# A quarter of the weights' low parts made by ScalarE and an adding transfer in place of VectorE's subtraction

## The chip, the cores and the metric

The kernel runs on one core of a Trainium2 chip, and its time is the device time of one launch in microseconds. TensorE (PE in the profile; PEld is its weight load) multiplies matrices, VectorE (DVE), ScalarE (ACT) and GpSimd (POOL) do the rest, SyncE (SP) issues transfers. Each engine works through its own list of instructions in order and waits on semaphores where it needs another's result. A transfer that GpSimd issues goes through a queue of its own (q0 in the profile), one that SyncE issues through another (q1).

## The reference

One step of a two-layer trunk over 128 context tokens and 512 latent tokens, width 1024, all in float32. Cut to what matters here:

```
h = rms(x, norm1) * (1 + sc1) + sh1
proj = h @ w_in                      # 1024 -> 8464 columns, split below
qa, ka, va, ga, beta, alpha, qb, ib, fb, gb, q_c, k_c, v_c, mg = split(proj)
o_a = rms(gated_delta(q, k, v, ...)) * silu(ga)      # recurrence over chunks of 64
o_b = rms(hgrn2(silu(qb), ib, fb, ...)) * silu(gb)   # recurrence over chunks of 32
o_c = windowed_attention(q_c, k_c, v_c)
x = x + g1 * (sum_r sigmoid(mg_r) * (o_r @ w_branch_r)) @ w_out
h2 = rms(x, norm2) * (1 + sc2) + sh2
x = x + g2 * (silu(conv(h2 @ w_up_a)) * conv(h2 @ w_up_u)) @ w_down
```

## The kernel before

TensorE multiplies in a reduced format (float32r), so every product is made of three: activations and weights are each split into a high part, which the format holds exactly, and a low part, the rest. A step over 128 rows of a weight block (k_steps, line 969) does high weights x high activations, high weights x low activations, low weights x high activations, each in two pieces of 256 and 384 tokens.

Weights come in blocks of four such steps, 128 x 512 numbers, 256 KB. SyncE loads a block into wraw (w_issue, line 897), ScalarE copies it into whi in the reduced format, and VectorE subtracts: wlo = wraw - whi (the function go in w_queue, line 927). There are four buffers each of wraw, whi and wlo (NRAW and NHI, lines 41 and 42). A block's high part is queued once the block four before it has been used up, so TensorE has three other blocks to work on in the meantime; a raw buffer is loaded again once its block has been split. The blocks of the first three tiles of layer 1 and of each ConvFFN have buffers of their own (wx) and are split twelve blocks early (W_EARLY).

The program is written in one pass by a planner. Several streams (the projections as the main one; two for the delta recurrence, one for the other recurrence, and attention, norms and adaLN beside them) each hand out their next instructions. A model clock for each engine (_go, _ready) says when a stream could go on, and drive (line 512) takes a stream that is ready by TensorE's clock, or else the next projection step. So the order of every engine's list, TensorE's included, is fixed when the kernel is built, and depends on what the planner believes of each operation's cost. In a mixer the projections of w_in for the heads a0 a1 b0 a2 b1 a3 b2 b3 (MIX_ORDER, line 51) are the filler between the steps of the recurrences; then come the attention columns, the gates ga and gb, and the merge with mg. VectorE does the recurrences' elementwise work, the short convolutions (Cv) and the subtractions, all in one queue. POOL issues the spills of the context tokens' part (pspill), the loads of states and part of the adaLN weights, and sets a few buffers to zero.

Of the kernel before, what the change touches and what calls it, by code (L numbers as in the profile page):

```python
# [7 lines left out]
F32 = mybir.dt.float32  # L8
# [3 lines left out]
AF = mybir.ActivationFunctionType  # L12
ALU = mybir.AluOpType
# [19 lines left out]
ENGS = ("pe", "act", "dve", "pool")  # L33
# [3 lines left out]
PRIO = {"norm": -1, "ab": 0, "attn": 3, "ada": 4, "y": 0}  # L37
PRIO_MIX = ({"delta": 1, "delta1": 2, "hgrn": 2}, {"delta": 1, "delta1": 2, "hgrn": 2})
ADA_LATE = 3000.0
C_ROOM = (5, 5)  # L40
NRAW = 4
NHI = 4
# [15 lines left out]
IN_COL = {"q": 0, "k": 512, "v": 1024, "ga": 1536, "ab": 2048, "qb": 2064, "ib": 2576,  # L58
          "ff": 3088, "fb": 3600, "gb": 4112, "qc": 4624, "kc": 5136, "vc": 5264, "mg": 5392}
# [177 lines left out]
class Trunk:  # L237
# [181 lines left out]
    def dma(self, out, in_, queue="pool", fresh=False):  # L419

        load = self.in_sbuf(out)
        e, n = ENGS.index("pool"), len(ENGS)
        c = self._cells(out if load else in_)
        t = 0.0 if fresh else self._ready(e, [c] if load else [], [] if load else [c])
        t = max(self.clk[queue], t) + (1050.0 if queue == "pool" else 450.0)
        self.clk[queue] = t
        self.clk["dma"] = max(self.clk["dma"], t) + out.shape[0] * self._n(out) / 90.0
        t = self.clk["dma"] + 2000.0
        if load:
            c[e] = t  # L430
        else:
            np.maximum(c[n + e], t, out=c[n + e])
        (self.nc.gpsimd if queue == "pool" else self.nc.sync).dma_start(out=out, in_=in_)  # L433
        return t

    @staticmethod
    def in_sbuf(ap):
# [318 lines left out]
    def ada_rest(self, chunks, raws, accs, gap, done, after=None):  # L756
# [15 lines left out]
        for n, (l, j, k) in enumerate(steps):  # L772
# [10 lines left out]
            if k < KD - 1 or not q:  # L783
                continue
            self.cur.now += ADA_LATE
            yield None
# [3 lines left out]
            self.cp(ar, ps)  # L790
            self.cur.now += ADA_LATE
            yield None
# [115 lines left out]
    def w_queue(self):  # L908

        if self.w_queued == len(self.units):  # L910
            return False
        u = self.w_order[self.w_queued]
        key, _, _, kt, n, own = self.units[u]
        if own:
            if self.wx is None:
                return False
            hi, lo = self.wx[:, own - 1, 0], self.wx[:, own - 1, 1]
        else:
            if len(self.w_ring) >= NHI and self.w_ring[-NHI] >= self.w_free:
                return False  # L920
            self.w_ring.append(u)
            hi = self.rotating(self.wp, [128, 4, 128], "whi", NHI, F32R, bufs=NHI)
            lo = self.rotating(self.wp, [128, 4, 128], "wlo", NHI, F32R, bufs=NHI)
        n = max(n, 32)
        self.w_hl[u] = (hi, lo)

        def go():
            raw = self.w_rawt.pop(u)
            if n < 128:
                self.cp(hi[:, :kt, :n].bitcast(F32), raw[:, :kt, :n])  # L930
            else:
                self.cp(hi[:, :kt, :n], raw[:, :kt, :n])
                self.sub(lo[:, :kt, :n], raw[:, :kt, :n], hi[:, :kt, :n].bitcast(F32))
            self.w_done.add(u)

        self.w_pend.append(go)
        self.w_queued += 1
        return True
# [968 lines left out]
    def mixer(self, l, x):  # L1907
# [71 lines left out]
        def c_tiles():  # L1979
            yield self.room(2, C_ROOM[l], sl)  # L1980
            self.qc = [sl.pair(), sl.pair()]
            self.qcp = sl.half()
            self.kv = [sl.half() for _ in range(3)]
            self.spawn("attn", self.attention(l))
            for i, n in enumerate(("kc", "vc")):
                yield from self.mtile(("in", l, IN_COL[n]), self.hh, self.hl, KD)
                self.cp(self.s2(self.kv[i].ap), self.s_view(self.ps))
                self.cp(self.kv[2].c4[:, i], self.p_view(self.ps))
            self.post(("Ck", l))
            for j in range(4):  # L1990
                yield from self.mtile(("in", l, IN_COL["qc"] + j * 128), self.hh, self.hl, KD)
                self.cp(self.s2(self.qc[j // 2].ap[:, j % 2]), self.s_view(self.ps))
                self.cp(self.qcp.c4[:, j], self.p_view(self.ps))
            self.post(("Cq", l))
# [333 lines left out]
```

## Time and profile before

| | |
|---|---|
| time, median of 3 runs | 2674.06 us (2673.45 to 2674.49) |
| profiled execution, its own time | 2671.22 us |
| its span | 2669.4 us |
| TensorE busy | 2634.9 us, 99% |
| VectorE busy | 1843.0 us, 69% |
| ScalarE busy | 1130.8 us, 42% |
| POOL busy | 114.4 us, 4% |

A share of busy time is a mean over stages. Matmuls overlap, so a busy TensorE may still lose a few tenths of a microsecond at a time while its next weight load waits; the view of waits counts these by what ended them. "issue" is time in which an engine waited for nothing that the profile shows.

### The profile page before, as it was taken

What the parts mean: (1) busy time and instruction counts of PE and PEld (TensorE: products, weight loads), DVE (VectorE), ACT (ScalarE), POOL (GpSimd) and SP (SyncE); (2) the same over time, 40 slices, a digit from 0 to 9 for tenths busy, and PEclk for the clock granted to TensorE, in tenths of its full rate; (3) what the DMA queues carried; (4) which work ended last, traced back from release to release, by engine and by line L of the source; (5) the groups of instructions that cost most, each with busy time, mean ns of one, the idle gap of its engine ahead of it and who ended that gap; (6) DMA issues with size and microseconds to landing.
All of it is one profiled execution on the core that took longest, in us unless ns stands there. A gap on an engine that the chain in (4) does not pass through costs nothing.

```text
span 2669.4 us, 58665 instructions
## 1 busy us (share of the span) xinstructions
PE 2634.9 (99%) x23938; PEld 2534.1 (95%) x23938; DVE 1843.0 (69%) x4250; ACT 1130.8 (42%) x2577; POOL 114.4 (4%) x208
## 2 busy tenths in 40 slices
PE   8999999999999999999999999999999999999999
PEld 5999999999999999999999998999999999999999
DVE  6788865656765897988667888666564457546454
ACT  5555455544424432323345554645443334323232
POOL 1100110100000000000001001000000000000000
PEclk9999999999999999999999999999999999999999
DMA  8212222312444344444322112222222232222222
GB/s 270 73 40 58 65 75 80 112 53 60 134 132 131 100 141 154 151 149 148 108 77 75 44 49 63 65 71 66 56 64 68 76 115 68 77 74 69 83 74 81
DMA packets 365245, 243.49 MB, mean 91 GB/s; under 512 B 18069, under 2 KB 339137, under 8 KB 364848
## 3 DMA queue, kind: packets, MB, share of 16 engines
q1 hardware_dynamic: 355632, 213.70, 27.7%
q0 software_dynamic: 8912, 25.53, 2.9%
q8 instruction: 188, 3.08, 0.5%
q14 instruction: 81, 0.66, 0.1%
q10 hardware_dynamic: 432, 0.52, 0.1%
HBM read 225.79 MB, written 13.89 MB: 90 GB/s over the span
## 4 chain that ended last, share of the span: by engine, by line
PE 88%; DVE 7%; ACT 2%; issue 2%; DMA 1%; SPq 0%; ACTq 0%; DVEq 0%
PE mm L323 73%; PE sd L323 12%; PE sd L328 2%; DVE sl L358 1%; DVE ex L358 1%; DVE Cv L371 1%; ACT sl L348 1%; DMA ar<-in_ada_w_dram 1%; DVE acc L371 1%; DVE wlo L358 1%; DMA wraw<-in_w_up_dram 0%; DVE N L371 0%; SPq L433 0%; ACT ex L348 0%; DVE x L371 0%
## 5 line engine op out<-in xcount | busy, mean ns | idle before, releaser
L323 PE MATMUL mm<-hh,whi 128*128 128x256 f32 (+2 forms) x3696 | 868.7, 319 | 1.4 <-issue 0.7
L323 PE MATMUL mm<-hl,whi 128*128 128x256 f32 (+2 forms) x3696 | 840.4, 311 | 1.2 <-DVE hl L371 1.2
L323 PE MATMUL mm<-hh,wlo 128*128 128x256 f32 (+1 forms) x3632 | 834.8, 309 | 0.0
L323 PEld LDWEIGHTS mm<-hh,whi 128*128 128x128 f32 (+1 forms) x3696 | 646.1, 187 | 23.8 <-issue 15.4
L323 PEld LDWEIGHTS mm<-hl,whi 128*128 128x128 f32 (+1 forms) x3696 | 663.7, 187 | 4.0 <-DVE hl L371 1.8
L323 PEld LDWEIGHTS mm<-hh,wlo 128*128 128x128 f32 x3632 | 661.7, 188 | 0.0
L358 DVE TENSOR_TENSOR wlo<-wraw,whi 128x512 fp32r<-128x512 f32 x598 | 401.8, 681 | 302.6 <-ACT whi L348 301.8
L348 ACT ACTIVATE whi<-wraw 128x512 fp32r<-128x512 f32 x602 | 366.8, 618 | 306.7 <-PE mm L323 245.6
L371 DVE SCALAR_TENSOR_TENSOR Cv<-S,V,Cv 128x642 f32<-128x642 f32 x240 | 210.9, 886 | 2.3
L371 DVE SCALAR_TENSOR_TENSOR acc<-ar,cT,acc 128x512 f32<-128x512 f32 x252 | 176.8, 749 | 4.2 <-DMA ar<-in_ada_w_dram 4.0
L348 ACT ACTIVATE sl<-sl 128x512 f32<-128x512 f32 (+5 forms) x220 | 117.6, 545 | 143.5 <-DVE sl L358 103.3
L323 PE MATMUL mm<-fh,whi 128*128 128x256 f32 (+1 forms) x704 | 166.0, 311 | 1.8 <-DVE x L371 1.0
L323 PE MATMUL mm<-fl,whi 128*128 128x256 f32 (+1 forms) x704 | 165.0, 309 | 0.2
L323 PE MATMUL mm<-fh,wlo 128*128 128x256 f32 (+1 forms) x704 | 165.1, 309 | 0.0
L348 ACT ACTIVATE sl<-sd 128x512 f32<-128x512 f32 (+5 forms) x216 | 94.4, 451 | 161.7 <-PE sd L323 79.6
L323 PE MATMUL sd<-sl,sl 128*32 128x32 f32 (+4 forms) x3392 | 151.2, 228 | 6.3 <-DVE sl L358 5.1
L323 PEld LDWEIGHTS sd<-sl,sl 128*32 128x32 f32 (+3 forms) x3392 | 126.1, 129 | 26.8 <-issue 13.9
L358 DVE TENSOR_TENSOR sl<-sl,sl 128x512 f32<-128x512 f32 (+2 forms) x212 | 149.0, 741 | 3.3 <-ACT sl L348 2.0
L348 ACT ACTIVATE S<-mm 128x512 f32<-128x512 f32 x204 | 77.8, 434 | 155.0 <-PE mm L323 154.8
L371 DVE SCALAR_TENSOR_TENSOR x<-mm,mod,x 128x256 f32<-128x256 f32 (+1 forms) x192 | 74.6, 434 | 88.2 <-PE mm L323 83.8
L323 PEld LDWEIGHTS mm<-fh,whi 128*128 128x128 f32 x704 | 128.0, 189 | 4.2 <-issue 2.9
L323 PEld LDWEIGHTS mm<-fl,whi 128*128 128x128 f32 x704 | 128.1, 188 | 0.7 <-DVE fl L358 0.7
(280 smaller groups left out, 3121.6 us busy)
## 6 DMA issues: line engine op xcount, KB each, us to landing
wraw<-in_w_in_dram SPq DMA_DIRECT2D x264, 256.0 KB, 3.0
ar<-in_ada_w_dram SPq DMA_DIRECT2D x176, 256.0 KB, 3.5
wraw<-in_w_up_dram SPq DMA_DIRECT2D x176, 256.0 KB, 3.0
wraw<-in_w_down_dram SPq DMA_DIRECT2D x64, 256.0 KB, 3.0
wraw<-in_w_branch_dram SPq DMA_DIRECT2D x48, 256.0 KB, 3.0
wraw<-in_w_out_dram SPq DMA_DIRECT2D x32, 256.0 KB, 3.6
wraw<-in_w_down_dram SPq DMA_DIRECT2D x32, 192.0 KB, 2.6
x<-xspill POOLq DMA_DIRECT2D x16, 320.0 KB, 7.0
```

What stands on the lines that cost most here:

```text
L323: self.nc.tensor.matmul(out, lhsT, rhs, start=start, stop=stop)
L328: self.nc.tensor.transpose(out, in_, self.c_i[:k, :k])
L348: self.nc.scalar.activation(out=out, in_=in_, func=func, scale=scale, bias=bias, **kw)
L358: self.nc.vector.tensor_tensor(out, a, b, op=op)
L371: self.nc.vector.scalar_tensor_tensor(out=out, in0=a, scalar=s, in1=b, op0=op0, op1=op1)
```

## The change

For a weight block of w_in whose column lies ahead of the attention keys (columns of q, k, v, ga, qb, ib, ff, fb, gb and qc, without the first tile of q), the low part is made in another way: ScalarE writes the negative high part into wlo (a copy with scale -1.0), and a transfer issued by POOL adds the raw block to it in place. Everything else keeps the subtraction. Of the 616 blocks that are split, 152 in wlo and 4 in wx are of the new kind. In the planner's clock an addition costs POOL 1050 ns, and its result is there 2500 ns later.

```
+BY_DMA = ("in",)
...
+    def dma_add(self, out, in_):
+
+        e, n = ENGS.index("pool"), len(ENGS)
+        oc, ic = self._cells(out), self._cells(in_)
+        t = max(self.clk["pool"], self._ready(e, [oc], [ic])) + 1050.0
+        self.clk["pool"] = t
+        oc[e] = np.maximum(oc[e], t + 2500.0)
+        np.maximum(ic[n + e], t + 2500.0, out=ic[n + e])
+        self.nc.gpsimd.dma_start(out=out, in_=in_, accum_op=ALU.add)
...
                 self.cp(hi[:, :kt, :n], raw[:, :kt, :n])
-                self.sub(lo[:, :kt, :n], raw[:, :kt, :n], hi[:, :kt, :n].bitcast(F32))
+                if key[0] in BY_DMA and key[2] < IN_COL["kc"] and key[2] != IN_COL["q"]:
+                    self.act(lo[:, :kt, :n], raw[:, :kt, :n], AF.Copy, scale=-1.0)
+                    self.dma_add(lo[:, :kt, :n].bitcast(F32), raw[:, :kt, :n])
+                else:
+                    self.sub(lo[:, :kt, :n], raw[:, :kt, :n], hi[:, :kt, :n].bitcast(F32))
```

Since the planner's clocks differ, the lists of all engines are ordered a little differently. On VectorE, at the first short convolution of layer 0 (S0, S1 and Cv2 are its inputs, Cv0, Cv1 and Cv3 its sums, V the taps, sc_ the scalars of the delta recurrence), the list before reads:

```order
L376 TENSOR_SCALAR sc_t0_659<-sc_ab_655 128x40
L358 TENSOR_TENSOR wlo_814<-wraw_625,whi_813 128x512
L371 SCALAR_TENSOR_TENSOR Cv0_81<-S0_79,V_85,Cv0_81 128x642
L358 TENSOR_TENSOR sc_t0_659<-sc_t0_659,sc_ab_655 128x40
L371 SCALAR_TENSOR_TENSOR Cv1_82<-S1_80,V_85,Cv1_82 128x642
L371 SCALAR_TENSOR_TENSOR Cv0_81<-S0_79,V_85,Cv0_81 128x642
L371 SCALAR_TENSOR_TENSOR Cv1_82<-S1_80,V_85,Cv1_82 128x642
L358 TENSOR_TENSOR wlo_853<-wraw_715,whi_852 128x512
L376 TENSOR_SCALAR sc_t1_660<-sc_t0_659 128x40
L371 SCALAR_TENSOR_TENSOR Cv0_81<-S0_79,V_85,Cv0_81 128x642
L371 SCALAR_TENSOR_TENSOR Cv1_82<-S1_80,V_85,Cv1_82 128x642
```

And the same place now:

```order
L377 TENSOR_SCALAR sc_t0_662<-sc_ab_658 128x40
L359 TENSOR_TENSOR sc_t0_662<-sc_t0_662,sc_ab_658 128x40
L377 TENSOR_SCALAR Cv3_84<-Cv2_83,V_85 128x642
L377 TENSOR_SCALAR sc_t1_663<-sc_t0_662 128x40
L372 SCALAR_TENSOR_TENSOR Cv3_84<-Cv2_83,V_85,Cv3_84 128x642 x4
L379 TENSOR_SCALAR sc_t1_663<-sc_t1_663 128x40
L401 RECIPROCAL sc_t1_663<-sc_t1_663 128x40
L377 TENSOR_SCALAR Cv0_81<-S0_79,V_85 128x642
L377 TENSOR_SCALAR sc_t2_664<-sc_t2_664 128x40
L372 SCALAR_TENSOR_TENSOR Cv0_81<-S0_79,V_85,Cv0_81 128x642
```

The subtractions that stood between the taps and the scalar steps are gone, and the taps of one convolution stand closer together.

On POOL, in the same part of layer 0 (pspill takes the context tokens' part of a convolution or projection, st00 is a state that is loaded), the list before reads:

```order
L433 DMA pspill<-Cv0_81 128x128
L433 DMA pspill<-Cv1_82 128x128
L433 DMA pspill<-Cv3_84 128x128
L433 DMA st00_652<-in_state_delta_dram 128x128 x2
L433 DMA pspill<-Cv0_81 128x128
L433 DMA pspill<-pst_1164 128x128
L433 DMA pspill<-pst_1254 128x128
```

And now, where each wlo row is an addition:

```order
L445 DMA wlo_827<-wraw_628 128x512
L445 DMA wlo_864<-wraw_719 128x512
L434 DMA pspill<-Cv0_81 128x128
L445 DMA wlo_902<-wraw_745 128x512
L445 DMA wlo_942<-wraw_791 128x512
L434 DMA pspill<-Cv1_82 128x128
L434 DMA pspill<-Cv3_84 128x128
L445 DMA wlo_982<-wraw_831 128x512
L434 DMA pspill<-Cv0_81 128x128
L445 DMA wlo_1028<-wraw_868 128x512
L445 DMA wlo_1060<-wraw_906 128x512
L445 DMA wlo_1109<-wraw_946 128x512
```

Each spill and each load of a state now has additions ahead of it and behind it in POOL's queue.

## Rows read from the trace of the kernel before

**Rows 1.** the page's part 1: busy us, share of span, instructions.

```profile
PE 2634.9 (99%) x23938; PEld 2534.1 (95%) x23938; DVE 1843.0 (69%) x4250; ACT 1130.8 (42%) x2577; POOL 114.4 (4%) x208
```

**Rows 2.** the page's part 4: the chain that ended last.

```profile
PE 88%; DVE 7%; ACT 2%; issue 2%; DMA 1%; SPq 0%; ACTq 0%; DVEq 0%
```

**Rows 3.** windows: both recurrence stretches, columns in the first line.

```profile
core 0: us, PE busy (x) PEld busy (x) DVE busy (x) ACT busy (x) POOL busy (x), PEclk, DMA share, GB/s
50.00:450.00 400.00, 396.16 (x5488) 370.07 (x5488) 304.29 (x841) 209.44 (x513) 38.35 (x68) 1.00 0.24 64
1385.00:1800.00 415.00, 407.82 (x5608) 383.20 (x5607) 325.88 (x883) 219.62 (x536) 38.69 (x69) 1.00 0.24 63
```

**Rows 4.** waits of weight loads, 50 to 450: total, times, longest.

```profile
PEld sd L323 <- DVE ex L358: 2.8, 13, 0.4
PEld sd L323 <- DVE sl L358: 2.1, 8, 0.4
PEld sd L323 <- ACT sl L348: 1.4, 6, 0.3
```

**Rows 5.** waits of weight loads, 1385 to 1800 us.

```profile
PEld sd L323 <- ACT sl L348: 3.2, 12, 0.9
PEld sd L323 <- DVE sl L358: 2.7, 5, 1.9
PEld sd L323 <- DVE ex L358: 1.8, 8, 0.3
```

**Rows 6.** the page's part 5: count, busy, mean ns, idle before.

```profile
L358 DVE TENSOR_TENSOR wlo<-wraw,whi 128x512 fp32r<-128x512 f32 x598 | 401.8, 681 | 302.6 <-ACT whi L348 301.8
L348 ACT ACTIVATE whi<-wraw 128x512 fp32r<-128x512 f32 x602 | 366.8, 618 | 306.7 <-PE mm L323 245.6
L371 DVE SCALAR_TENSOR_TENSOR Cv<-S,V,Cv 128x642 f32<-128x642 f32 x240 | 210.9, 886 | 2.3
```

**Rows 7.** groups of VectorE, 50 to 450 us.

```profile
L358 DVE TENSOR_TENSOR wlo<-wraw,whi 128x512 fp32r<-128x512 f32 x69 | 46.9, 686 | 34.0 <-ACT whi L348 33.9
```

**Rows 8.** groups of VectorE, 1385 to 1800 us.

```profile
L358 DVE TENSOR_TENSOR wlo<-wraw,whi 128x512 fp32r<-128x512 f32 x73 | 49.2, 686 | 41.5 <-ACT whi L348 41.3
```

**Rows 9.** groups of POOL, whole span.

```profile
L433 POOL DMA_DIRECT2D pspill<-pst x32 | 17.4, 543 | 251.5 <-ACT pst L348 200.3 <-DVE sc_ssb L358 20.3 <-DVE sl L371 8.2
```

**Rows 10.** timeline of ScalarE and POOL at 301: start, duration, idle before.

```profile
300.93 0.27 ACT L348 ACTIVATE pst<-mm 128x128 f32<-128x128 f32 x1
301.50 0.54 POOL L433 DMA_DIRECT2D pspill<-pst  x1 [5.06 <-ACT pst L348]
```

**Rows 11.** transfers: issues, KB each, median us to landing.

```profile
wraw<-in_w_in_dram SPq DMA_DIRECT2D x264, 256.0 KB, 3.0
x<-xspill POOLq DMA_DIRECT2D x16, 320.0 KB, 7.0
ar<-in_ada_w_dram POOLq DMA_DIRECT2D x16, 256.0 KB, 4.2
sl<-pspill POOLq DMA_DIRECT2D x14, 256.0 KB, 4.0
xspill<-x POOLq DMA_DIRECT2D x6, 320.0 KB, 2.4
```

**Rows 12.** the page's part 3: the queue that POOL feeds.

```profile
q0 software_dynamic: 8912, 25.53, 2.9%
```

**Rows 13.** timeline at layer 1's start, ScalarE and weight loads.

```profile
1386.61 1.18 ACT L348 ACTIVATE whi<-wraw 128x512 fp32r<-128x512 f32 x2
1390.18 0.36 PEld L323 LDWEIGHTS mm<-hh,wlo 128*128 128x128 f32 x2
```

**Rows 14.** timeline at 1776 us, ScalarE and weight loads.

```profile
1776.04 1.14 ACT L348 ACTIVATE whi<-wraw 128x512 fp32r<-128x512 f32 x2
1782.27 0.36 PEld L323 LDWEIGHTS mm<-hh,wlo 128*128 128x128 f32 x2
```

**Rows 15.** waits of SyncE's queue, whole span.

```profile
SPq L433 <- DVE wlo L358: 1863.4, 511, 31.2
```

## The prediction

> **What bounds the kernel now.** I read the page's busy table first: TensorE is busy for 99% of the span and VectorE for 69% [rows 1]. The chain that ended last says the same from the other side: 88% of it is TensorE and 7% VectorE [rows 2]. So the question is not how much VectorE work goes away, but how much TensorE time is spent waiting for VectorE. The windows view cuts out the two stretches in which the recurrences run beside the moved weight blocks, 50 to 450 us (layer 0) and 1385 to 1800 us (layer 1). There VectorE is busy for 304 of 400 us and 326 of 415 us, ScalarE for 209 and 220 us, and the granted clock is 1.00 [rows 3]. The waits of TensorE's weight loads come next, since every matmul stands behind one. In the first stretch those ended by VectorE come to 6.4 us, over rows of which the two largest are shown (2.8 and 2.1 us), and those ended by ScalarE to 3.1 us [rows 4]. In the second they come to 7.9 and 4.2 us [rows 5]. Together: 14.3 us behind VectorE, 7.3 us behind ScalarE. This is all that a lighter VectorE can give back in these stretches; the rows ended by "issue" are short gaps at the change from one matmul shape to another, and no engine's load moves them.
>
> **What is removed.** 156 subtractions (152 into wlo, 4 into wx) leave VectorE. One takes 681 ns on the page [rows 6], so 156 x 0.681 = 106 us leave 1843 us of VectorE work. In the stretches nearly all subtractions are moved ones: 69 cost 46.9 us and held VectorE's queue for another 34.0 us waiting for the high part [rows 7], 73 cost 49.2 and 41.5 us [rows 8]. VectorE's occupied time in the first stretch falls from 304 + 34 = 338 to about 260 of 400 us. In the order of VectorE's rows the conv taps now follow each other where a subtraction stood between them. What does TensorE gain? At most the 14.3 us; at least nothing, since TensorE's order is fixed and the recurrence is a chain in which the next wait may end only a little earlier. I take half, -7 us, because the queue's load falls by about a quarter and the waits are short ones (0.2 to 0.4 us for most of them), which end either with the queue or with the chain itself.
>
> **What is added on ScalarE.** 156 copies of the form of whi<-wraw at 618 ns [rows 6]: 97 us, of which some 43 us fall in each stretch, on an engine that is busy for about 53% there [rows 3]. Queued behind each copy are the ScalarE steps of the recurrences and the evacuations of the accumulators. If ScalarE's waits grow with its load, by a fifth, the 7.3 us grow by +1 us; the bound above is a doubling, +7 us, below nothing.
>
> **What is added on POOL and the transfer queue.** 156 issues. A transfer issue on POOL took 543 ns, for all 32 of one kind [rows 9]. POOL has 38 us of work in each stretch [rows 3], so it can take 40 us more. It works in order, and an addition stands behind spills, state loads and memsets. I put each of these beside the next high part in the code's order: in the kernel before, POOL was done with it at most 0.6 us after that high part was written, except for the adaLN loads and state stores around the attention tiles; the spill of pst shows the usual case, POOL idle for 5.06 us until ScalarE is done [rows 10]. So I cost the queue at nothing. What waits behind an addition on POOL are the spills of Cv and pst, which have tens of microseconds until they are read back.
>
> The low part now arrives later. Before: high part 0.62 us, subtraction 0.69 us. After: high part 0.62, negative copy 0.62, then 0.30 us from ScalarE's end to POOL's start (pst ends at 300.93 + 0.27 = 301.20, the issue starts at 301.50 [rows 10]), then issue to landing. No row shows an accumulating transfer within SBUF, so I bound it by the rows of POOL's transfers: 2.4 us (320 KB to HBM, alone) below, 7.0 us (320 KB, eight at once) above; the rows nearest to it in size and direction are 4.0 and 4.2 us (256 KB into SBUF) [rows 11]. It has to read a second operand. The queue's packets took 2.9% of 16 engines' span for 25.53 MB [rows 12], which is 0.029 x 2669 x 16 / 25.53 = 48.5 us of one engine per MB, or 0.8 us for 0.26 MB over 16 engines. I take 4.0 + 0.8 = 4.8 us. From the start of the high part to the low part: 0.62 + 0.62 + 0.30 + 4.8 = 6.34 us.
>
> The Trainium skill, "Collectives: The Full Stack", section "The bandwidth ceiling: the fold count and why AG ≠ RS ≠ AR", says the same of an adding transfer: the add itself is free, but it reads two sources and moves half as fast. "DMA: Bandwidth & Descriptors", section "Anatomy of one DMA — SWDGE (gpsimd) path", gives 2.0 us plus bytes over 436e3 per us for a transfer issued by GpSimd, 2.6 us for 256 KB; this trace disagrees for the same size (4.0 and 4.2 us [rows 11]), and by that figure with its data part doubled (3.2 us) the late low parts below would cost 2 us, not 9.
>
> How much time is there? For every moved block I matched, by their place in the engines' orders, the start of the high part with TensorE's first use of its low part. The median over the 63 blocks of the first stretch is 14.2 us, so most arrivals are hidden behind the three blocks that TensorE does in between. Seven blocks have less than 6.34 us: 3.57, 4.38, 4.39, 5.13, 5.75, 6.06 and 6.23 us. The shortest is at the start of layer 1 (high part at 1386.61, first use at 1390.18 [rows 13]), the last at 1776.04 (first use at 1782.27 [rows 14]). They are late by 2.77, 1.96, 1.95, 1.21, 0.59, 0.28 and 0.11 us, in all 9 us, and TensorE, in order, can do nothing else meanwhile. At 2.4 us to landing (3.94 from the high part) only the first is late, 0.4 us; at 7.0 us (8.54) twenty are, and with what an earlier stall gives back to the next ones it is 38 us.
>
> A raw block is held until the addition has landed, some 5 us longer, and SyncE, in order, waits for it: VectorE's subtraction is what it waited for in 511 of its issues, 1863 us in total [rows 15]. That costs nothing by my count, since a load lands in 3.0 us [rows 11] and the shortest time from a load's issue to its high part is 6 us in these stretches, the usual one 13 to 25 us; with the cover gone it would be a few tenths at the layer starts.
>
> TensorE does the same 19669 matmuls, with 806 changes between projection and recurrence where there were 810: nothing.
>
> **Sum.** -7 (waits behind VectorE) + 1 (ScalarE) + 9 (late low parts) = +3 us on the profiled execution's 2671.22 us: 2674. The median of the runs lies 2.8 us above that execution, so 2677 us. About 0.2%, or 5.3 us, is what a measurement of this kernel can tell from no change; +3 us is inside it.
>
> **Rivals.**
> *VectorE was the brake.* All 14.3 us of waits go and the transfers land in about 3 us (1 us late): -14 + 1 + 1 = -12, 2662 us. For it: the subtractions hold VectorE's queue for 34 and 41 us with nothing done [rows 7, 8]. Against it: TensorE's wait rows are so small.
> *The addition is slow.* Landing takes 7.0 us: -7 + 1 + 38 = +32, 2706 us. It decides from about 5.2 us to landing, where the late parts cost 12 us and the sum passes +5. For it: the 7.0 us row, raw loads on the same engines, and additions that come in pairs. Against it: the 4.0 us rows.
> *VectorE holds up POOL's issue.* If an issue had to sit out one VectorE instruction such as the conv tap of 886 ns [rows 6], the path grows to 7.2 us, twelve blocks are late, 18 us in all: +12, 2686 us. Against it: the POOL issues in the busiest VectorE stretches lasted 543 ns on average like any other [rows 9]. The Trainium skill, "SBUF — State Buffer", section "Who interferes with whom", speaks against the change here: a VectorE instruction in a two-port mode keeps GpSimd from writing descriptors. By the page's figures for it, 3.1 us in place of 0.62, the path would be 8.8 us; the trace so far shows no such issue.
>
> **How the numbers follow.** No measurable change 0.42 (its own range 2669 to 2679), VectorE as the brake 0.28, the slow addition 0.25, POOL's issue held up 0.05. So faster 0.28, same 0.42, slower 0.30. The range is 2660 to 2704 us: it takes in the first rival but for its best corner, and the slow addition up to nearly 7.0 us.
>
> **What would show it.** In the profile after: VectorE near 1737 us and ScalarE near 1227 us busy; POOL with 156 issues more; a row wlo<-wraw among the transfers with its time to landing, 4.8 us by my sum; waits of TensorE's loads ended by that transfer at the layer starts and in the gate tiles, some 9 us; VectorE-ended waits near 7 us. Landing below 3.5 us or above 6 us, or VectorE-ended waits that vanish or stay at 14 us, would make the forecast wrong; so would stalls at spills behind a held POOL queue.

## The result, and the profile after

The changed kernel takes 2689.38 us (median of 4 runs, 2685.88 to 2693.12) where the kernel before takes 2674.27 (2673.45 to 2674.95) beside it: ratio 1.0059 [1.0045, 1.0074], some 15 us slower. The range held it, but by luck: its upper end was set by a slow addition, which did not come, and the likeliest case, no measurable change, did not come either. The profiled execution took 2691.9 us.

Part 1 of the page after, against [rows 1]:

```profile
PE 2640.7 (98%) x23938; PEld 2539.3 (94%) x23938; DVE 1754.2 (65%) x4094; ACT 1208.2 (45%) x2731; POOL 252.3 (9%) x364
```

VectorE lost 156 instructions and 89 us, ScalarE gained 77 us, GpSimd 138 us: the change does what it says (1754.2 and 1208.2 us, where 1737 and 1227 were forecast). GpSimd's is more than its 156 issues suggest. Its groups after (as [rows 9]), the transfers (as [rows 11]: issues, KB, median us to landing) and the queue that it feeds (as [rows 12]: packets, MB, share of 16 engines):

```profile
L445 POOL DMA_DIRECT2D wlo<-wraw x152 | 133.6, 879 | 766.8 <-ACT wlo L349 460.0 <-DVE sl L377 102.1 <-PE sd L324 74.6
L434 POOL DMA_DIRECT2D pspill<-pst x32 | 19.5, 610 | 104.5 <-ACT pst L349 83.8 <-DVE ex L372 9.0 <-DVE sl L372 7.2
```

```profile
wlo<-wraw POOLq DMA_DIRECT2D x152, 256.0 KB, 3.7
...
ar<-in_ada_w_dram POOLq DMA_DIRECT2D x16, 256.0 KB, 5.2
sl<-pspill POOLq DMA_DIRECT2D x14, 256.0 KB, 5.1
...
q0 software_dynamic: 31376, 66.43, 12.0%
```

An issue takes 879 ns, not 543. The addition lands in 3.7 us, sooner than the 4.8 I reckoned with. But its neighbours on GpSimd's queue land later: the reload of a spilled tile in 5.1 us where it took 4.0, the adaLN load in 5.2 where it took 4.2. And the queue's share of the transfer engines went from 2.9% to 12.0%.

The windows of the two stretches (columns as in [rows 3]), and that of layer 0's gates and attention between them:

```profile
50.00:450.00 400.00, 394.52 (x5444) 369.68 (x5443) 267.00 (x776) 244.87 (x585) 95.61 (x132) 1.00 0.49 107
450.00:650.00 200.00, 193.51 (x1476) 180.57 (x1476) 120.38 (x326) 102.07 (x240) 24.07 (x33) 0.98 0.37 94
1385.00:1800.00 415.00, 404.43 (x5512) 380.02 (x5510) 285.62 (x819) 245.20 (x588) 91.49 (x128) 1.00 0.45 98
```

VectorE is 37 and 40 us lighter in the recurrences, yet TensorE gets no more done there; and the stretch that the prediction leaves out, 450 to 650 us, shows a mean granted clock of 0.98, where the kernel before has 1.00 and TensorE busy throughout:

```profile
450.00:650.00 200.00, 200.00 (x1519) 190.31 (x1518) 127.70 (x340) 100.03 (x238) 13.66 (x22) 1.00 0.29 82
```

The largest waits of weight loads that VectorE and ScalarE end, 50 to 450 us (as [rows 4]) and 1385 to 1800 us (as [rows 5]):

```profile
PEld sd L324 <- DVE ex L359: 2.4, 9, 0.7
PEld sd L324 <- DVE ex L372: 2.0, 7, 0.6
...
PEld sd L324 <- ACT sl L349: 1.2, 5, 0.3
```

```profile
PEld sd L324 <- DVE ex L359: 3.5, 12, 0.7
PEld sd L324 <- ACT sl L349: 2.6, 9, 0.5
PEld sd L324 <- ACT ex L349: 2.2, 7, 0.5
```

They are no smaller than before; other steps of the chains stand in the rows. SyncE's loads now wait for the transfer where they waited for VectorE (as [rows 15]):

```profile
SPq L434 <- DVE wlo L359: 1322.6, 402, 31.2
SPq L434 <- DMA wlo<-wraw: 779.4, 150, 15.8
```

Where the time goes is seen best by a count: the weight loads of the projections (14,576 of them, tiles mm) come in the same order in every kernel here, so the time of the n-th one in two traces can be subtracted. This gives the lag behind the kernel before, in us, in the profiled execution of each kernel (the last rows belong to the experiments below). The profiled execution of the kernel before was a fast one, 2671.22 us against medians of some 2675 beside the experiments, so a row shows where time is lost; how much a kernel loses is said by the medians further down.

| weight load (time in before) | 1800 (455) | 2400 (570) | 3900 (827) | 7200 (1342) | 7500 (1395) | 9000 (1768) | 10500 (2050) | last (2664) |
|---|---|---|---|---|---|---|---|---|
| changed kernel | 2.7 | 16.5 | 14.1 | 14.0 | 18.6 | 21.4 | 20.3 | 20.7 |
| new order, subtraction | 13.1 | 23.8 | 21.1 | 21.2 | 21.1 | 37.0 | 36.1 | 36.4 |
| new order, no low parts | 0.7 | 9.9 | 7.1 | 7.1 | 7.1 | 7.7 | 6.3 | 6.7 |
| old order, copy and transfer | 8.1 | 8.7 | 9.5 | 9.6 | 13.0 | 13.4 | 14.5 | 14.7 |
| old order, no low parts | 1.8 | 1.8 | 1.8 | 1.8 | 1.8 | 0.7 | -0.5 | -0.4 |
| old order, copy, unread transfer | 8.7 | 8.7 | 8.7 | 8.8 | 10.4 | 9.6 | 9.7 | 9.8 |
| the same, a quarter of the bytes | 2.7 | 2.7 | 2.8 | 2.8 | 2.8 | 0.6 | 0.7 | 0.7 |

The changed kernel loses nearly all of layer 0's 14 us between 455 and 570 us, another 4.6 at the start of layer 1, and little elsewhere.

### The profile page after: what moved, and what is told of

It is laid out like the page before. It is cut to its first block, busy times and chain, and to the rows that moved or that the text cites. A ratio compares the mean times of both kernels' runs of the same rounds, so it can differ in the third digit from the quotient of the medians.

```text
span 2690.1 us, 58982 instructions
## 1 busy us (share of the span) xinstructions
PE 2640.7 (98%) x23938; PEld 2539.3 (94%) x23938; DVE 1754.2 (65%) x4094; ACT 1208.2 (45%) x2731; POOL 252.3 (9%) x364
## 4 chain that ended last, share of the span: by engine, by line
PE 68%; issue 23%; DVE 3%; DMA 3%; ACT 2%; POOL 1%; SPq 0%; POOLq 0%; DVEq 0%; ACTq 0%
PE mm L324 55%; PE sd L324 11%; PE sd L329 2%; DMA ar<-in_ada_w_dram 1%; ACT sl L349 1%; DVE sl L359 1%; DMA wlo<-wraw 1%; DMA wraw<-in_w_up_dram 0%; SPq L434 0%; DVE sl L414 0%; ACT ex L349 0%; DVE ex L359 0%; DVE Cv L372 0%; DVE sl L377 0%; ACT whi L349 0%
## 5 line engine op out<-in xcount | busy, mean ns | idle before, releaser
L359 DVE TENSOR_TENSOR wlo<-wraw,whi 128x512 fp32r<-128x512 f32 (+1 forms) x446 | 299.2, 678 | 256.0 <-ACT whi L349 255.6
L445 POOL DMA_DIRECT2D wlo<-wraw x152 | 133.6, 879 | 766.8 <-ACT wlo L349 460.0
L324 PE MATMUL sd<-sl,sl 128*32 128x32 f32 (+6 forms) x3368 | 148.9, 228 | 3.8 <-issue 1.8
L324 PEld LDWEIGHTS sd<-sl,sl 128*32 128x32 f32 (+2 forms) x3368 | 124.5, 128 | 24.2 <-issue 10.7
```

The lines of the kernel that those rows point to most:

```text
L324: self.nc.tensor.matmul(out, lhsT, rhs, start=start, stop=stop)
L359: self.nc.vector.tensor_tensor(out, a, b, op=op)
L445: self.nc.gpsimd.dma_start(out=out, in_=in_, accum_op=ALU.add)
```

## The experiments

All 12 ran in 4 to 11 runs each, beside runs of the kernel before on the same chip (medians 2674.9 to 2675.4). Two things come with the change that the diff shows as one: another way to get the low part, and, since the planner reckons with its costs, other lists for every engine. The planner's reckoning and the instruction issued can be set apart, so that each is had without the other. In the traces VectorE, ScalarE and GpSimd do all their other work in e2, e5, e6, e7, e9 and e10 in exactly the order of the kernel before, and in e1, e4 (its moved loads apart) and e12 in that of the changed kernel.

| kernel | order of the lists | low parts of the 156 blocks | median us | ratio to before, 95% |
|---|---|---|---|---|
| e1 | new | VectorE subtracts | 2707.34 | 1.0122 [1.0107, 1.0138] |
| e2 | old | copy and transfer | 2690.64 | 1.0053 [1.0040, 1.0066] |
| e3 | a third | as changed, but 48 blocks subtracted | 2684.95 | 1.0041 [1.0029, 1.0054] |
| e4 | new | as changed; 16 adaLN loads' issues on SyncE | 2688.52 | 1.0051 [1.0039, 1.0064] |
| e5 | old | none | 2670.49 | 0.9980 [0.9971, 0.9989] |
| e6 | old | copy alone, unread | 2672.03 | 0.9988 [0.9979, 0.9997] |
| e7 | old | copy and transfer, unread | 2683.36 | 1.0031 [1.0019, 1.0043] |
| e8 | a fourth | VectorE subtracts (before, in all it does) | 2689.65 | 1.0052 [1.0040, 1.0065] |
| e9 | old | GpSimd subtracts | 2705.19 | 1.0116 [1.0100, 1.0132] |
| e10 | old | as e7, a quarter of the bytes | 2675.72 | 1.0001 [0.9992, 1.0010] |
| e11 | a fifth | VectorE subtracts (before, in all it does) | 2679.43 | 1.0013 [1.0004, 1.0022] |
| e12 | new | none | 2677.94 | 1.0015 [1.0006, 1.0024] |

**e1, the new order alone.** The planner is told of the copy and the transfer, and VectorE is given the subtraction (a, b and c are low part, raw block and high part here and below).

```diff
-                    self.act(lo[:, :kt, :n], raw[:, :kt, :n], AF.Copy, scale=-1.0)
-                    self.dma_add(lo[:, :kt, :n].bitcast(F32), raw[:, :kt, :n])
+                    a, b, c = lo[:, :kt, :n], raw[:, :kt, :n], hi[:, :kt, :n].bitcast(F32)
+                    self._go("act", 0.833 * self._n(b) + 93, [a], [b])
+                    self.dma_add(a.bitcast(F32), b)
+                    self.nc.vector.tensor_tensor(a, b, c, op=ALU.subtract)
...
-        self.nc.gpsimd.dma_start(out=out, in_=in_, accum_op=ALU.add)
```

> Every instruction list in the changed kernel's order (its planner reckons with the copy on ScalarE and the transfer on GpSimd), but VectorE subtracts as before and no transfer adds. Theory O (the new order of the lists makes the loss of 15 us): 2684 to 2692 us, the lag behind the kernel before again built up between 450 and 570 us of the span. Theory M (the copies on ScalarE and the adding transfers on GpSimd's queue make it, whatever the order): 2669 to 2679 us, since VectorE's time goes back to some 1840 us and GpSimd issues 156 transfers fewer than the changed kernel.

2707.34 us, beyond both. Lists laid out for a VectorE that is free of the subtractions pay when it is not; waits of TensorE's loads in this kernel, 50 to 450 us:

```profile
PEld sd L324 <- DVE ex L372: 8.0, 11, 2.0
PEld sd L324 <- DVE ex L359: 3.6, 12, 0.7
```

The pair is 3.7 us in the kernel before. So this run alone can't price the order. Its lag does say one thing: between 455 and 570 us it loses 10.7 us with no transfer in it.

**e2, the new low parts alone.** The planner is told of the subtraction.

```diff
-                    self.act(lo[:, :kt, :n], raw[:, :kt, :n], AF.Copy, scale=-1.0)
-                    self.dma_add(lo[:, :kt, :n].bitcast(F32), raw[:, :kt, :n])
+                    self._dve(a, 1.04, b, c)
+                    self.nc.scalar.activation(out=a, in_=b, func=AF.Copy, scale=-1.0, bias=0.0)
+                    self.nc.gpsimd.dma_start(out=a.bitcast(F32), in_=b, accum_op=ALU.add)
```

> Every instruction list in the order of the kernel before (its planner reckons with a subtraction on VectorE), but the low parts of the 156 blocks come from ScalarE's negative copy and the adding transfer. Theory O (order): 2670 to 2680 us, the low parts alone costing TensorE the 3 to 6 us that the changed kernel's trace gives to waits for the transfer. Theory M (mechanism): 2684 us or more, and with lists that were not laid out for it up to 2700 us.

2690.64 us: the mechanism loses 14 us by the ratio (1.0053) with the lists untouched, as theory M says. And it does not lose them where the changed kernel does: 0.6 us between 455 and 570 us, but 8.1 us before that.

**e3, no additions in the gates.**

```diff
-                if key[0] in BY_DMA and key[2] < IN_COL["kc"] and key[2] != IN_COL["q"]:
+                if key[0] in BY_DMA and key[2] < IN_COL["gb"] and not IN_COL["ga"] <= key[2] < IN_COL["qb"] and key[2] != IN_COL["q"]:
```

> The changed kernel with 48 of its 156 blocks (the two gates' and the attention's query columns) given back to VectorE's subtraction, so that no adding transfer runs in the stretch from 450 to 570 us where layer 0 lost 14 us; the planner lays the lists out anew for it. Theory G (the loss sits in the gate and attention stretch): 2672 to 2680 us. Rival (each of the 156 blocks costs its share of 15 us, 0.1 us each): 2684 to 2686 us.

2684.95 us, the rival's figure, but not by its mechanism. The lag is 2.1 us all through layer 0, as theory G wants, and then grows by 11 us in layer 1, where lists and additions are other ones again and where some of it is clock (the mean granted clock is 0.997 in this profile, 1.000 in that of the kernel before). Inconclusive as a price; it shows that each set of lists loses in places of its own.

**e4, adaLN loads off GpSimd's queue.**

```diff
-        (self.nc.gpsimd if queue == "pool" else self.nc.sync).dma_start(out=out, in_=in_)
+        (self.nc.gpsimd if (by or queue) == "pool" else self.nc.sync).dma_start(out=out, in_=in_)
...
-                                 "pool" if gap else "sync")
+                                 "pool" if gap else "sync", by="sync")
```

> The changed kernel, order as it is, with the 16 adaLN weight loads that stood on GpSimd's queue among the adding transfers issued from SyncE. Theory Q (adding transfers stand behind these loads, which wait for their buffers; TensorE's waits for low parts around 460 us come from that): 2680 to 2686 us, with TensorE's waits for the transfer between 450 and 650 us at under 0.5 us instead of 1.7 us. Rival (the queue's order does not matter, or SyncE's raw loads now stand behind the same waits): 2687 us or more.

2688.52 us: the rival. The wait for a low part (1.7 us in the changed kernel) is gone between 450 and 650 us, and a wait of 1.6 us for an adaLN load stands in its place; the lag still grows by 9 us there.

**e5, e6, e7, e10: the mechanism a piece at a time, in the old order.** TensorE reads the high part in place of the low one, so that the low part's lateness has no price; e5 is the first two lines, e6 adds the third, e7 the fourth, and e10 has the fifth in place of the fourth.

```diff
+                    self._dve(a, 1.04, b, c)
+                    self.w_hl[u] = (hi, hi[:, :, :])
+                    self.nc.scalar.activation(out=a, in_=b, func=AF.Copy, scale=-1.0, bias=0.0)
+                    self.nc.gpsimd.dma_start(out=a.bitcast(F32), in_=b, accum_op=ALU.add)
+                    self.nc.gpsimd.dma_start(out=a[:, :1].bitcast(F32), in_=b[:, :1], accum_op=ALU.add)
```

> Leaves out the low parts of the 156 blocks: in the order of the kernel before, VectorE's 156 subtractions are gone, nothing stands in for them, and TensorE's matmuls on a low part read the block's high part instead (as many matmuls, of the same shapes). So it shows what VectorE's relief is worth at most. My prediction's term (half of the waits that VectorE ends): 2664 to 2669 us. Rival R (VectorE was the brake): 2662 us or less. Theory N (VectorE's time was hidden but for a microsecond or two, as the changed kernel's waits say): 2670 to 2675 us.

2670.49 us, theory N's interval. VectorE's relief is worth 0.20% [0.11, 0.29], 5 us: some 70% of the 7 I gave it, and no brake. The waits of TensorE's loads that VectorE ends show it: 4.6 + 4.2 = 8.8 us in the two stretches, where the kernel before has 14.3.

> As the kernel without low parts, with ScalarE's negative copy of the 156 blocks put in (TensorE still reads the high part, nothing waits for the copy but its buffers). The step over the kernel without low parts is what ScalarE's load costs. My prediction's term: 1 to 2 us. Rival: 4 us or more, since VectorE and ScalarE take turns in the recurrences' chains.

2672.03 us: +1.5 us for 156 copies on ScalarE, in the middle of my 1 to 2 (the intervals of e5 and e6 overlap).

> As the kernel with the copy, with the adding transfer put in as well; TensorE still reads the high part, so no matmul waits for a low part. The step over the kernel with the copy is what GpSimd's issues, the queue and the raw buffers' longer hold cost; what the full mechanism in the same order (2690.6 us) has over it is the late low parts. Theory T (the transfers slow the reloads and loads beside them): a step of 5 us or more, as the wait of 2.8 us for a spilled tile in the mechanism's run suggests. Theory W (late low parts): a step within 2 us here, and 5 us or more left to the full mechanism.

2683.36 us: the transfers alone cost 11.3 us, though nobody reads what they add. Theory T. The full mechanism has 7.3 us over this one by the medians, 6 by the ratios, for the low parts that come late and for a lower granted clock in three of its five runs (more on that below).

> As the kernel with the copy and the unread adding transfer (2683.4 us), but each transfer adds only a quarter of the block, 64 KB instead of 256 KB; the low parts are left out of the result as there. As many issues on GpSimd, each waiting for ScalarE's copy as before, a quarter of the bytes. Theory B (the bytes of the adding transfers slow the transfers beside them): the step of 11.3 us over the copy alone falls to 3 to 4 us, so 2675 to 2676 us. Theory Q (GpSimd's list in order: each add waits there for the copy, and the spills and reloads stand behind it): 2680 to 2684 us.

2675.72 us: 3.7 us over the copy alone, theory B. GpSimd's list and the packets are the same in both; the bytes differ. Group of the additions and queue, first e10, then e7:

```profile
L949 POOL DMA_DIRECT2D wlo<-wraw x152 | 133.5, 878 | 733.9 <-ACT wlo L948 476.0 <-DVE sl L377 179.9 <-ACT Cv L349 28.9
...
q0 software_dynamic: 31376, 35.76, 6.3%
```

```profile
L949 POOL DMA_DIRECT2D wlo<-wraw x152 | 133.3, 877 | 735.8 <-ACT wlo L948 466.1 <-DVE sl L377 179.9 <-ACT Cv L349 28.9
...
q0 software_dynamic: 31376, 66.43, 12.0%
```

As many issues of the same length, held up for as long by ScalarE's copy: GpSimd's list is not it, beyond at most the 3.7 us that e10 still has over the copy alone. What lands later with the bytes are above all the small neighbours on the queue. Over the whole span, e10:

```profile
sl<-pspill POOLq DMA_DIRECT2D x14, 256.0 KB, 4.2
...
pspill<-Cv POOLq DMA_DIRECT2D x24, 64.0 KB, 2.0
```

And e7:

```profile
sl<-pspill POOLq DMA_DIRECT2D x14, 256.0 KB, 4.3
...
pspill<-Cv POOLq DMA_DIRECT2D x24, 64.0 KB, 3.0
```

The spill of Cv takes 1.9 us in e6, without additions. The large neighbours do not go by the bytes in general: the reloads of spilled tiles land in 3.8 us in e6 and all but equally late in e10 and e7, and the adaLN loads land in 4.9 us in e6, 5.7 in e10 and 5.1 in e7. TensorE waits for such a neighbour in one place, the reload of a spilled tile between 300 and 460 us; the waits of its loads and the transfers there, e10:

```profile
PEld sd L329 <- DMA sl<-pspill: 0.4, 1, 0.4
...
sl<-pspill POOLq DMA_DIRECT2D x4, 256.0 KB, 5.5
```

And e7:

```profile
PEld sd L329 <- DMA sl<-pspill: 1.8, 1, 1.8
...
sl<-pspill POOLq DMA_DIRECT2D x4, 256.0 KB, 6.9
```

A second path may be the raw buffer, which is held until its addition has landed, so that SyncE's next load starts late. ScalarE's waits for raw blocks over the whole span, e10 and then e7:

```profile
ACT whi L349 <- DMA wraw<-in_w_in_dram: 3.8, 3, 2.4
...
ACT whi L349 <- DMA wraw<-in_w_down_dram: 1.2, 1, 1.2
```

```profile
ACT whi L349 <- DMA wraw<-in_w_in_dram: 7.8, 6, 3.5
...
ACT whi L349 <- DMA wraw<-in_w_down_dram: 5.2, 3, 2.2
```

With the blocks of the other weights ScalarE's waits for raw blocks come to 11.3 us in e10 and 19.9 in e7, but to 16.7 in e6, where nothing is held for an addition, so these waits are no price by themselves. A quarter of the bytes also lands sooner (2.4 us instead of 3.7), so e10 shrinks both, the load on the transfer engines and the hold; no run here parts them, and by which path the bytes cost their 7.6 us (2683.36 - 2675.72) stays open. Nor do the direct waits come to that much: most of the rest stands in e7's trace as longer gaps that end with "issue", VectorE or ScalarE in the recurrences, and I can't follow it link by link.

**e8, e11: other lists, same work.** The kernel before, its planner reckoning 1.00 (e8) or 1.08 ns (e11) per element in place of 1.04 for the 156 subtractions (the diff, e8's, is against the changed kernel).

```diff
-                    self.act(lo[:, :kt, :n], raw[:, :kt, :n], AF.Copy, scale=-1.0)
-                    self.dma_add(lo[:, :kt, :n].bitcast(F32), raw[:, :kt, :n])
+                    self._dve(lo[:, :kt, :n], 1.0, raw[:, :kt, :n], hi[:, :kt, :n].bitcast(F32))
+                    self.nc.vector.tensor_tensor(lo[:, :kt, :n], raw[:, :kt, :n], hi[:, :kt, :n].bitcast(F32), op=ALU.subtract)
```

> The kernel before in all it does, every operation as it was, but its planner reckons 1.00 instead of 1.04 ns per element for the 156 subtractions (20 ns of some 600 each), so that it lays the lists out anew. Theory P (a new layout is worth several us by itself, in either direction): more than 4 us from 2674.9 us. Rival (a layout that fits its operations is worth the same, and only one laid out for other operations loses): 2672 to 2678 us.

> The kernel before in all it does, every operation as it was, but its planner reckons 1.08 instead of 1.04 ns per element for the 156 subtractions, so that it lays the lists out anew once more. Theory P (a new layout is worth several us by itself, in either direction; 1.00 ns gave 2689.7 us): more than 4 us from 2675 us, above or below. Rival (too light a cost loses, a slightly heavy one does not): 2673 to 2679 us.

2689.65 and 2679.43 us: theory P, though e11's 4 us only just. A reckoning off by 20 ns in some 600 moves this kernel by up to as much as the whole change does, with every operation as it was. Waits of TensorE's loads in e8, 50 to 450 us, and then 1385 to 1800 us (against [rows 4, 5]):

```profile
PEld sd L329 <- DVE ex L359: 4.5, 2, 3.6
PEld sd L324 <- DVE ex L372: 3.2, 5, 1.6
```

```profile
PEld sd L324 <- ACT ex L349: 6.5, 5, 2.9
```

In the first stretch single waits of 1.6 and 3.6 us stand where the kernel before has none for VectorE above 0.4; in the second one of 2.9 us for ScalarE, where its longest was 0.9: chains that TensorE reaches too early.

**e9, GpSimd subtracts.** Could VectorE's relief be kept without a transfer?

```diff
+                    self._dve(a, 1.04, b, c)
+                    self.nc.gpsimd.tensor_tensor(a, b, c, op=ALU.subtract)
```

> The order of the kernel before, but the 156 low parts are subtracted on GpSimd: no copy on ScalarE, no transfer, VectorE's 156 operations gone. If the 4.8 us that VectorE's relief is worth can be kept and only the low parts come later, 2671 to 2675 us. Rival: GpSimd's list now holds some 150 to 200 us of subtractions in front of its spills and reloads, or its operations slow VectorE's beside them: 2680 us or more.

2705.19 us, the rival. GpSimd's group, and VectorE's conv tap from 50 to 450 us beside it:

```profile
L947 POOL TENSOR_TENSOR wlo<-wraw,whi 128x512 fp32r<-128x512 f32 x152 | 213.7, 1410 | 673.6 <-ACT whi L349 449.7 <-PE mm L324 178.5 <-PE sd L324 29.6
```

```profile
L372 DVE SCALAR_TENSOR_TENSOR Cv<-S,V,Cv 128x642 f32<-128x642 f32 x32 | 33.7, 1072 | 0.0
```

GpSimd takes 1.41 us where VectorE took 0.68, and VectorE's tap grows from 883 ns in that stretch of the kernel before (886 over its span [rows 6]) to 1072: VectorE is busy for 1854.6 us in e9, more than before, with 156 operations fewer. The Trainium skill, "SBUF — State Buffer", section "Who interferes with whom", says that a VectorE instruction with two inputs in SBUF contends with a GpSimd instruction that reads SBUF; this trace agrees.

**e12, the new order with nothing in it.** The planner is told of the copy and the transfer, as in e1; nothing is issued for them, and the matmuls that planned with lo read hi.

```diff
-                    self.act(lo[:, :kt, :n], raw[:, :kt, :n], AF.Copy, scale=-1.0)
-                    self.dma_add(lo[:, :kt, :n].bitcast(F32), raw[:, :kt, :n])
+                    self._go("act", 0.833 * self._n(b) + 93, [a], [b])
+                    self.dma_add(a.bitcast(F32), b)
+                    self.bare[id(lo)] = (hi, lo)
...
+                        real=self.bare[id(lo)][0][:, k % 4, :] if wt is lo and id(lo) in self.bare else None)
...
-        self.nc.gpsimd.dma_start(out=out, in_=in_, accum_op=ALU.add)
```

> The order of the changed kernel, with the low parts of the 156 blocks left out altogether: no copy, no transfer, no subtraction, and TensorE reads the high part in their place. Its counterpart in the order of the kernel before took 2670.5 us, so the difference between the two is what the new layout costs with nothing of the mechanism in it, and what the changed kernel (2689.4 us) has over it is the mechanism. Theory O (the layout loses in layer 0's gates and attention, some 7 us without the clock's part): 2677 to 2682 us, and the mechanism costs 8 to 12 us in this layout, less than the 20.1 us it costs in the old one. Rival (the layout fits VectorE's relief and keeps what it is worth): 2671 us or less, and the mechanism costs 18 us or more here too.

2677.94 us: theory O. Against e5 the new lists cost 7.4 us by the medians (0.35% by the ratios, 9 us, give or take 3), and the mechanism in them costs the rest of the way to 2689.4, 11.4 us. Waits of TensorE's loads, 450 to 650 us, in e5 (old order), e12 and the changed kernel:

```profile
PEld mm L324 <- issue: 3.9, 12, 0.8
...
PEld sd L324 <- ACT Cv L349: 0.2, 1, 0.2
```

```profile
PEld mm L324 <- issue: 5.3, 14, 0.8
PEld sd L329 <- DVE acc L359: 3.1, 1, 3.1
...
PEld mm L324 <- ACT Cv L349: 2.0, 2, 1.1
```

```profile
PEld mm L324 <- issue: 5.7, 15, 0.8
PEld sd L329 <- DVE acc L359: 3.1, 1, 3.1
...
PEld mm L324 <- ACT Cv L349: 2.3, 3, 1.1
PEld mm L324 <- DMA wlo<-wraw: 1.7, 1, 1.7
```

In the new order TensorE comes to its transposes (L329) of the other recurrence's output before VectorE has normed it. The norm's scalars are sc_ssb, worked through in small steps, and the wait of 3.1 us ends with an adaLN sum (acc) that stands right behind the norm in VectorE's list; from the changed kernel's timeline:

```profile
491.10 0.69 DVE L359 TENSOR_TENSOR sl<-sl,sc_ssb 128x512 f32<-128x512 f32 x1
491.70 0.41 DVE L359 TENSOR_TENSOR acc<-acc,sd 128x256 f32<-128x256 f32 x1
...
492.17 1.36 PEld L329 LDWEIGHTS sd<-cst,sl 128*128 128x128 f32 x7 [3.09 <-DVE acc L359]
```

It also comes twice to an accumulator that ScalarE has not yet emptied into Cv (2.0 us). The old order has neither wait. The changed kernel has both, and on top the one that is the mechanism's own. No kernel here that makes all low parts beats the kernel before.

## Why the prediction was right or wrong

**"-7 us", VectorE's relief: about right, but only in the old order.** e5 gives -4.8 us, the interval -3 to -8. In the changed kernel the waits ended by VectorE in the two stretches stayed where they were (14.3 us before; 6.4 + 7.1 = 13.5 after, summed as in [rows 4, 5]), one of the prediction's own signs of being wrong. Nor were the rows ended by "issue" out of every load's reach, as the prediction has it: the largest grew from 8.6 to 10.2 us and from 10.6 to 12.5.

**"+1 us", ScalarE: right.** e6: +1.5 us.

**"+9 us", late low parts: over-reckoned.** The landing took 3.7 us, not 4.8. From the start of the high part to the landing it is 5.2 us at the median in the changed kernel, not 6.34, and the direct waits of TensorE's loads for the addition come to 3.7 us in e2 and 3.4 us in the changed kernel. The 7.3 us that e2 has over e7 by the medians look like the 9, but are not all lateness. At a mean granted clock of 0.999 e2's two runs (2682.60 and 2685.93 us) lie 1.4 us above the mean of e7's five (2682.85); e2's other three ran at 0.997 (2690.64 to 2692.27). In the two profiled executions, both at 0.999, e2 ends 4.9 us behind e7. So the late parts cost some 1 to 5 us, and whether they also make the clock fall is not shown. The block I named as the shortest is late in the changed kernel, e2 and e4; waits around layer 1's start after (against [rows 13]):

```profile
PEld mm L324 <- DMA wlo<-wraw: 1.2, 1, 1.2
```

**"I cost the queue at nothing" and the raw buffer's hold "costs nothing by my count": this step failed.** The transfers cost 11.3 us in e7 with no reader. I looked at who stands behind whom on GpSimd, and there nothing was about right (in the changed kernel an addition starts 0.29 us after ScalarE's copy at the median, over 1 us after it for 7 of 152). I priced the addition's own landing; I did not price what 152 transfers of 256 KB do to the landing of others, though I had the queue's figures in hand [rows 12] and used them only for the addition itself. e10 puts 7.6 of the 11.3 us on the bytes and what hangs on them; by which path is open.

**"806 changes between projection and recurrence where there were 810: nothing": this step failed too.** The two counts are right (the profile has 23938 matmuls in either kernel, not the prediction's 19669), but they say nothing of whether a chain is ready when TensorE reaches it. e12 against e5: +7.4 us by the medians; 9.2 us are lost from 455 to 570 us, of which 2.8 come back by 827. I priced only the two stretches where the moved blocks lie thickest, and the loss is between them.

**The sum.** Forecast: -7 + 1 + 9 + 0 + 0 = +3. Measured, by medians: -4.8 (relief) + 7.4 (new lists) + 11.4 (mechanism in these lists) = +14.0, against 2675.4 beside e12; the changed kernel stands at 2689.4. The mechanism costs 20.1 us in the old lists (1.5 + 11.3 + 7.3) and 11.4 in those laid out for it: 8.7 us less, while the new lists lose 7.4 elsewhere. Part of the 8.7 is e2's lower clock: between the means of the runs at 0.999 the mechanism costs 14.8 and 9.4 us. Whether the planner wins the rest by knowing of the transfers, or by the scatter of lists that e8 and e11 show, no run tells.

**Rivals.** VectorE as the brake (2662): refuted by e5, which has no transfers at all and is at 2670.5. The slow addition (2706): landing is 3.7 us. GpSimd's issue held up by VectorE (2686): the additions' issues took 879 ns each, more than the 543 I had, but the 3.7 us to landing are counted from the issue's start, and e10, with as many issues of that length, is at 2675.7, 3.7 us over the copy alone. So the issue isn't where most of the time went. A time near 2686 came for other reasons.

**The spread.** The changed kernel's four runs go with TensorE's mean granted clock: 2685.88 and 2686.85 us at 0.999, 2691.9 and 2693.1 at 0.997 and 0.996. In the profiled one the granted clock is low in the slice in which the 3.1 us wait ends at 492.17 us (columns as in [rows 3]):

```profile
480.00:490.00 10.00, 9.02 (x72) 7.77 (x70) 8.33 (x31) 6.03 (x19) 4.55 (x9) 1.00 0.33 106
490.00:500.00 10.00, 7.83 (x37) 7.83 (x38) 6.37 (x16) 4.74 (x11) 2.44 (x4) 0.66 0.64 191
```

A mean of 0.66 is some 7 of the 10 us at the lower of the two levels (1.2 GHz instead of 2.4); 10 us do the work of 6.6, so 3.4 us are lost beside a wait of 3.1. The profiled executions of e12 and e4 have the same wait and stayed at 1.00 around it; that is the larger part of why their lag grew by 9 us there where the changed kernel's grew by 14. Where the clock fell in the runs without a profile, and what decides it, these runs don't show. The clock is in other kernels' medians too: e12's runs at 0.997 took 2680.91 to 2682.38 us, those at 0.999 took 2675.68 to 2677.94. What the new lists lose is not clock alone: between the means of the runs at 0.999, e12 is 7.5 us over e5.

## What to carry to other kernels

A planner's new costs are two changes, an operation and a new order of everything; run the old order with the new operation, and the new order with the operation left out, before explaining either, and price the order's own scatter (here 4 and 14 us, the latter with some clock in it, for a hair in one cost) before believing a gain or a loss of that size. Read the stretches between those that the change touches as well. A transfer that nobody waits for is not free: its bytes have to be in the sum, with what they may do to the landing of its neighbours and to the buffers it holds.

## What I had not expected of the hardware

- An adding transfer of 256 KB within SBUF landed in 3.7 us and one of 64 KB in 2.4 us (medians of 152 each); plain ones of 256 KB on the same queue, which come from DRAM and stand several in a row, took 4.0 and 4.2 us [rows 11]. The Trainium skill, "Collectives: The Full Stack", section "The bandwidth ceiling: the fold count and why AG ≠ RS ≠ AR", has the adding step of a collective run at half the rate of a copy, since it reads two sources; no run here has a plain copy of a block within SBUF beside the addition, so these runs neither show that nor speak against it.
- Its issue kept GpSimd for 0.88 us whatever the bytes (879, 877 and 878 ns), and other issues grew beside it: that of pst's spill from 543 to 610 ns.
- 156 subtractions moved to GpSimd made VectorE as a whole busier (1854.6 us against 1843.0), by lengthening what ran beside them.
